# Taking the value and key weights of the second half 512 columns at a time, with another opening and another final sum

## The chip, the cores and the metric

One core of one Trainium2 chip. The metric is the device time of one launch, in microseconds (us): the median over runs of the same kernel. The engines are named as in the profile: PE (TensorE matmul), PEld (its weight load), DVE (VectorE), ACT (ScalarE), POOL (GpSimd) and SP (SyncE, which here issues the DMAs).

## The reference

One layer of a hybrid encoder in fp32, on a prompt of 2048 frames and a sample of 64 frames with 4096 cached ones, 1024 channels.

```python
h = rmsnorm(x, norm_g) @ w_in                     # 1024 -> 6144 columns
qa, ka, va, za, qb, kb, vb, zb, ga, gb = split(h) # 512 each, ga and gb 1024
# branch A: 4 heads, two 64-wide parts each, softmax(p0) - lam * softmax(p1), ALiBi, chunk mask
oa = diff_attention(rmsnorm(qa), rmsnorm(ka), va)
# branch B: 4 heads of retention, chunks of 64, a decaying state
ob, state = retention(qb, kb * 128 ** -0.5, vb)
m = sigmoid(ga + b0) * ((rms(oa) * silu(za)) @ w_oa) + sigmoid(gb + b1) * ((rms(ob) * silu(zb)) @ w_ob)
y = x + m @ w_out
```

The outputs are y for prompt and sample, the new keys and values, and the retention states.

## The kernel before

Every product with x or a weight is done in three fp32r matmuls on split operands: a high part (the cast to fp32r) and a low part (what the cast left off), hi·hi, hi·lo and lo·hi. The high part of a weight piece is cast on ACT (`w_piece`, tiles `wh`), the low part subtracted on POOL, for a few pieces on DVE (`w_low`, tiles `wl`). Pieces come from memory into `ws` tiles (`w_load`), issued on SP's queue.

The prompt is worked in two halves of 1024 rows; half 0 also carries the 64 sample rows. For each half, a stream `w_stream` goes through the columns of `w_in`: values, keys and queries of the attention, values of the retention (`natural`: a tile of 128 rows of x is loaded into PE as the stationary operand, and 256 or 512 columns of weights move past it), then the retention's queries and keys and the gates (`transposed`: weights stationary). Each output tile is handed to finishing work (`spawn_fin`: normalisation, splitting, storing). A second stream, `z_stream`, does the attention of half 0, the attention of the sample, the retention of half 0, and the attention and the retention of half 1. Where `w_stream` is done, `out_stream` follows: `m_tile` (the two output projections with `w_o_diff` and `w_o_ret`, 264 columns a matmul), then `y_quad` (the last product with `w_out`, seven block products instead of eight).

No order is written out for the whole: the streams are generators, and a planner with one clock for each engine, advanced by a cost for each instruction, decides at build time whose next step is emitted. `yield lambda: ...` holds a stream until the condition is met, `yield t` until PE's planned clock has reached t; `take` and `give` take and free one of a limited set of rooms by its tag. So an engine's instructions stand in a fixed order on the chip, and a change of a condition or a cost moves other streams' work too.

Places that the change touches:

- `opening` does the first row tile by a list, `OPENING`: H is x high by weight high, X is x low by weight high, L is x high by weight low, each with one of 8 chunks; T is the transposing of x tile 1 (`x_tile`). `warm(n)` emits n small matmuls on a tile of ones, whose result nobody uses.
- In half 1 of before, `ORD` gives the order of 256-column groups: values 0, keys 0, queries 0, a mark, values 1, keys 1, queries 1, a mark. With 256 columns two row tiles share a tile of 512 columns in PSUM.
- `w_room` says where split weights live: the ordinary rooms ("w", 16), or rooms of the attention ("K", "V") for the wide groups 0 and 2 (values and queries of half 0).
- `head_in` holds the loading of an attention head until the mark of its group has been passed by 9000 ns on PE's planned clock.
- `y_last` ends the kernel: the last block product is split in two halves of 256 columns, each added to `xr` and stored.

Of the kernel before, what the change touches and what calls it, by code (L numbers as in the profile page):

```python
# [45 lines left out]
XFLY = 3  # L46
# [3 lines left out]
OPENING = [(k[0], int(k[1])) for k in ("H0 X0 H1 X1 H2 X2 L0 H3 X3 L1 H4 X4 L2 T1 H5 X5 L3 H6 X6 L4 "  # L50
                                       "H7 X7 L5 L6 L7").split()]
# [20 lines left out]
class Hybrid:  # L72
# [197 lines left out]
    def x_prep(self):  # L270
# [131 lines left out]
    def spread(self):  # L402
# [8 lines left out]
        self.warm(2)  # L411
# [51 lines left out]
    def x_tile(self, j, mid=None):  # L463
# [3 lines left out]
        for q in range(2):  # L467
# [19 lines left out]
            if q == 0 and mid:  # L487
                yield from mid()
# [48 lines left out]
    def w_piece(self, wait):  # L537
# [10 lines left out]
        return self.w_low(wide, n, st, h, l, th, tag, tags)  # L548

    def w_low(self, wide, n, st, h, l, t, tag, tags):  # L550
        th = t
        if n in (5, 7, 8):
# [53 lines left out]
    def opening(self, fin):  # L606
# [16 lines left out]
        self.norm_scale(0)  # L623
        yield lambda: len(self.xin) > 1
# [10 lines left out]
        for _ in range(7):  # L635
# [6 lines left out]
        for k, c in OPENING:  # L642
            if k == "T":
# [42 lines left out]
    def natural(self, half, fin, fresh=False, wide=False):  # L686
        if fresh and wide:
# [319 lines left out]
    def q_loader(self, half):  # L1007
        for h in range(4):
            yield from self.head_in(half, h)
# [3 lines left out]
    def head_in(self, half, h):  # L1013
        k = f"kqv{h // 2}{half}"
        yield lambda: k in self.done
        yield self.marks[k] + 9000

    def h_loader(self, half):
        for h in range(4):
            yield from self.head_in(half, h)  # L1020
# [899 lines left out]
    def y_quad(self, g):  # L1920
# [3 lines left out]
        for k, (bank, b, need, done) in enumerate(SEVEN):  # L1924
# [31 lines left out]
            if split:  # L1956
                for u in range(2):
# [7 lines left out]
                    self.spawn(self.y_last(q, ps, t, cols), 0)  # L1965
# [70 lines left out]
    def y_last(self, q, ps, t, cols):  # L2036
        yield lambda: "x12" in q
        yield max(t, q["x12"])
        x = self.xr[q["g"]][0]["12"]
        self.nc.vector.tensor_add(x[:, cols], ps[:, cols], x[:, cols])  # L2040
        yield self.V(256, max(t, self.pe))
# [95 lines left out]
    def w_stream(self):  # L2137
# [12 lines left out]
        first = ([wva, wk, wq, m0, m1], ORD(fva0, fva, fk, fq, m0, m1))  # L2150
# [18 lines left out]
        self.npiece = 0  # L2169
        self.opened = False  # L2170
# [22 lines left out]
    def mark(self, name):  # L2193
        yield lambda: True
        self.done.add(name)
        self.marks[name] = self.pe

    def z_stream(self):
        for half in range(2):
            yield lambda: f"kqv0{half}" in self.done  # L2200
# [143 lines left out]
```

## Time and profile before

| | before |
|---|---|
| median of 3 runs (us) | 1929.06 (1929.06 to 1929.89) |
| the profiled execution, own time / span (us) | 1930.11 / 1928.3 |
| PE, PEld busy (us) | 1919.0, 1709.7 |
| DVE, ACT, POOL busy (us) | 1132.9, 1004.7, 463.8 |
| DMA | 308.50 MB, mean 160 GB/s |

The span is the part of the execution that the profiler covers; the 1.8 us between it and the execution's own time lie around it. Matmuls are pipelined, so that their durations overlap: 100% for PE says that some matmul is always under way, not that PE couldn't do more in the time. The pace is read from the timeline, from one start to the next. In the timeline each row has the start in us, the duration, the engine, the line, the operation, output<-inputs by the program's names, the shape and, in brackets, idle time ahead of it with what ended it.

### The profile page before, as it was taken

The numbers are of one execution on the slowest core, as the hardware profiler recorded it, in microseconds if no ns is written. First come the engines' busy times: TensorE is split into PE (matmuls) and PEld (weight loads), VectorE is DVE, ScalarE is ACT, GpSimd is POOL, SyncE is SP. The second block draws the span as 40 slices with busy tenths as digits, with TensorE's granted clock in tenths as the row PEclk, the third lists the DMA queues.
The fourth block names the chain that finished last, engine by engine and source line by source line (L and its number), as shares of the span: only waits on it lengthen the run. The fifth ranks groups of instructions, "written<-read, shape, count | busy, mean of one in ns | idle before, by whom it ended". The sixth has DMA issues, their size and how long they took to land.

```text
span 1928.3 us, 32935 instructions
## 1 busy us (share of the span) xinstructions
PE 1919.0 (100%) x11626; PEld 1709.7 (89%) x11626; DVE 1132.9 (59%) x2794; ACT 1004.7 (52%) x2137; POOL 463.8 (24%) x365
## 2 busy tenths in 40 slices
PE   9999999999999999999999999999999999999999
PEld 7878899999889999999988888888889889999887
DVE  6553575635565345656856656646664339977664
ACT  6433676655445544545756756645664535554221
POOL 2320121212121223212102211221221526522442
PEclk9999999999999999999999999999999999999999
DMA  7647463425556887664334243363233758886542
GB/s 247 208 149 185 139 182 117 125 84 161 167 158 172 228 230 206 179 195 141 106 104 138 90 129 97 107 190 108 69 115 101 236 167 253 261 247 198 180 153 77
DMA packets 356343, 308.50 MB, mean 160 GB/s; under 512 B 65745, under 2 KB 313809, under 8 KB 356178
## 3 DMA queue, kind: packets, MB, share of 16 engines
q1 hardware_dynamic: 356178, 306.39, 53.5%
q8 instruction: 92, 1.51, 0.3%
q14 instruction: 73, 0.60, 0.1%
HBM read 201.38 MB, written 99.88 MB: 156 GB/s over the span
## 4 chain that ended last, share of the span: by engine, by line
PE 95%; DVE 2%; DMA 1%; ACT 1%; issue 0%; SPq 0%; DVEq 0%; ACTq 0%
PE mm L592 55%; PE s L1066 3%; PE s L1067 3%; PE at L1174 3%; PE pv L1154 2%; PE pv L1153 2%; PE pv L1152 2%; PE s L1949 1%; PE s L1951 1%; PE s L1950 1%; PE pv L1420 1%; PE pv L1533 1%; PE at L1523 1%; PE tp L789 1%; PE mm L1949 1%; PE mm L1951 1%
## 5 line engine op out<-in xcount | busy, mean ns | idle before, releaser
L592 PE MATMUL mm<-xh,wh 128*128 128x512 f32 (+2 forms) x1280 | 457.5, 357 | 0.0
L592 PE MATMUL mm<-xh,wl 128*128 128x512 f32 (+2 forms) x1280 | 452.4, 353 | 0.0
L592 PE MATMUL mm<-xl,wh 128*128 128x512 f32 (+2 forms) x1280 | 451.9, 353 | 0.0
L556 POOL TENSOR_TENSOR wl<-ws,wh 128x512 fp32r<-128x512 f32 x189 | 256.7, 1372 | 654.8 <-ACT wh L546 479.0
L592 PEld LDWEIGHTS mm<-xh,wl 128*128 128x128 f32 x1280 | 240.9, 188 | 31.2
L592 PEld LDWEIGHTS mm<-xh,wh 128*128 128x128 f32 x1280 | 241.3, 188 | 29.1
L592 PEld LDWEIGHTS mm<-xl,wh 128*128 128x128 f32 x1280 | 241.3, 189 | 28.9
L592 PE MATMUL mm<-wh,xh 128*128 128x256 f32 (+1 forms) x696 | 235.8, 339 | 0.5 <-ACT raw L754 0.3
L592 PE MATMUL mm<-wh,xl 128*128 128x256 f32 (+1 forms) x696 | 231.1, 332 | 0.0
L592 PE MATMUL mm<-wl,xh 128*128 128x256 f32 (+1 forms) x696 | 230.8, 332 | 0.0
L1189 DVE TENSOR_TENSOR atl<-at,ath 128x512 fp32r<-128x512 f32 (+1 forms) x144 | 93.0, 659 | 146.7 <-ACT ath L1187 146.7
L892 ACT COPY ev<-mm 128x512 f32<-128x512 f32 x140 | 71.2, 509 | 190.6 <-PE mm L592 149.8
L1105 ACT ACTIVATE row<-row,a_mx 128x1024 f32<-128x1024 f32 (+7 forms) x160 | 153.8, 963 | 5.0 <-DVE a_mx L1085 4.8
L1075 DVE CUSTOM_DVE_ANT_0 row<-s,dfar 128x512 f32<-128x512 f32 (+2 forms) x192 | 118.0, 630 | 58.7 <-PE s L1067 58.5
L592 PEld LDWEIGHTS mm<-wh,xh 128*128 128x128 f32 x696 | 131.9, 190 | 14.1 <-ACT raw L754 0.8
L592 PEld LDWEIGHTS mm<-wh,xl 128*128 128x128 f32 x696 | 131.8, 189 | 13.3
L592 PEld LDWEIGHTS mm<-wl,xh 128*128 128x128 f32 x696 | 132.0, 190 | 12.7
L546 ACT CAST wh<-ws 128x512 fp32r<-128x512 f32 x192 | 115.6, 617 | 47.3 <-PE mm L592 24.7
L1187 ACT CAST ath<-at 128x512 fp32r<-128x512 f32 (+1 forms) x144 | 78.5, 564 | 100.5 <-PE at L1174 97.5
L955 POOL TENSOR_TENSOR r_y<-r_y,r_sq 128x256 f32<-128x256 f32 x33 | 24.7, 748 | 426.0 <-DVE r_sq L952 164.3
L1066 PE MATMUL s<-K,q 128*128 128x512 f32 (+3 forms) x320 | 119.4, 377 | 0.0
L1067 PE MATMUL s<-K,q 128*128 128x512 f32 (+3 forms) x320 | 115.6, 363 | 0.0
(387 smaller groups left out, 4180.9 us busy)
## 6 DMA issues: line engine op xcount, KB each, us to landing
ws<-in_w_in_dram SPq DMA_DIRECT2D x192, 256.0 KB, 3.1
q<-qT SPq DMA_DIRECT2D x128, 128.0 KB, 3.0
V<-vN SPq DMA_DIRECT2D x24, 512.0 KB, 5.6
K<-kT SPq DMA_DIRECT2D x48, 256.0 KB, 4.2
xt<-in_x_prompt_dram SPq DMA_DIRECT2D x16, 512.0 KB, 5.5
kn<-in_cache_k_T_dram SPq DMA_DIRECT2D x32, 256.0 KB, 3.4
vc<-in_cache_v_diff_dram SPq DMA_DIRECT2D x32, 256.0 KB, 3.3
mT<-mo SPq DMA_DIRECT2D x64, 128.0 KB, 3.1
```

Source lines behind the costliest of these rows:

```text
L546: self.nc.scalar.copy(h, st)
L556: self.nc.gpsimd.tensor_sub(l, st, h.bitcast(F32))
L592: nc.tensor.matmul(ps, p, q, start=c == 0 and i == 0, stop=c == KC - 1 and i == 2)
L892: nc.scalar.copy(ev, ps)
L1066: nc.tensor.matmul(ps, q1s, kk, start=True, stop=False)
L1067: nc.tensor.matmul(ps, q2s, kk, start=False, stop=True)
L1075: nc.vector.tensor_tensor_reduce(out=units[k0 // 1024][:, k0 % 1024:k0 % 1024 + n], in0=ps, in1=tab, scale=-SLOPES[h], scalar=3.0e38, op0= ...
L1105: nc.scalar.activation(u, u, AF.Exp, bias=mx, scale=-1.0, accum_out=lp[:, k:k + 1])
L1152: nc.tensor.matmul(o, v0, ah[:, s0:s0 + n], start=kt == 0, stop=False)
L1174: nc.tensor.transpose(at[:, w:w + 128], src, self.ident)
L1187: nc.scalar.copy(ah[:, :w], at[:, :w])
L1189: nc.vector.tensor_sub(al[:, :w], at[:, :w], ah[:, :w].bitcast(F32))
```

## The change

1. In half 1, values and keys are each one group of 512 columns (`wva`, `wk`), with the queries in two groups of 256 behind them. The order is values, keys, mark `kv1`, queries 0, mark `q01`, queries 1, mark `q11`. The wide values' weights live in the attention's rooms, and wait until the attention of the sample no longer needs its own (`n_spv == 4`).
2. `head_in` waits for the mark of what it needs (for half 1 `kv1` for keys and values, `q01` or `q11` for queries), and besides until all finishing work that was spawned ahead of that mark has ended (`fins`, `before`).
3. Odd pieces of the queries' weights in half 1 have their low parts made on DVE.
4. The opening: two weight pieces are loaded ahead of x tile 1, its list begins with two H products and has single filler matmuls (W), and `warm` is called for three instead of two, and for three more behind the first x tile; x tile 1 is normalised behind it.
5. The final sum: `y_last` is called at once after each half of the columns, no longer spawned.

```diff
-OPENING = [(k[0], int(k[1])) for k in ("H0 X0 H1 X1 H2 X2 L0 H3 X3 L1 H4 X4 L2 T1 H5 X5 L3 H6 X6 L4 "
-                                       "H7 X7 L5 L6 L7").split()]
+OPENING = [(k[0], int(k[1])) for k in ("H0 H1 W1 X0 X1 L0 L1 W1 H2 X2 H3 X3 H4 X4 L2 T1 H5 X5 L3 "
+                                       "L4 H6 X6 H7 X7 L5 L6 L7").split()]
...
# x_prep
-            yield lambda: self.xfly < XFLY and (j < 2 or self.wloads >= 8)
+            yield lambda: self.xfly < XFLY and self.wloads >= (0, 2, 8)[min(j, 2)]
...
# w_load
+                    if self.wloads == 2:
+                        yield lambda: len(self.xin) > 1
...
# w_room
-        elif nw in (0, 2):
+        elif nw in (0, 2, 4):
+            if nw == 4:
+                yield lambda: self.n_spv == 4
             tags, pool, shape = ("K", "V"), self.ap, [128, 2, 512]
...
-        return self.w_low(wide, n, st, h, l, th, tag, tags)
+        return self.w_low(wide, n in (5, 7, 8) or not wide and nw == 6 and q % 2, st, h, l, th, tag, tags)
...
# opening
+        for _ in range(2):
+            low.append((yield from self.w_piece(False)))
+        for g in low:
+            yield from g
+        yield from self.x_tile(0)
+        self.warm(3)
         yield lambda: len(self.xin) > 1
         self.norm_sums(1)
+        self.norm_log(1)
         self.norm_mean(1)
-
-        def first():
-            yield from (yield from self.w_piece(False))
-
-        yield from self.x_tile(0, first)
-        self.norm_log(1)
...
# spawn_fin
-        self.spawn(done, 0, "w")
+        self.spawn(self.finish(done, len(self.fins)), 0, "w")
+        self.fins.append(False)
+
+    def finish(self, done, k):
+        yield from done
+        self.fins[k] = True
...
-    def head_in(self, half, h):
-        k = f"kqv{h // 2}{half}"
+    def head_in(self, half, h, names):
+        k = names[half].format(h // 2)
         yield lambda: k in self.done
+        yield lambda: all(self.fins[:self.before[k]])
         yield self.marks[k] + 9000
...
# y_quad, the last product
+                yield lambda: "x12" in q
...
-                    self.spawn(self.y_last(q, ps, t, cols), 0)
+                    self.y_last(q, ps, t, cols)
                     yield self.pe
...
     def y_last(self, q, ps, t, cols):
-        yield lambda: "x12" in q
-        yield max(t, q["x12"])
         x = self.xr[q["g"]][0]["12"]
         self.nc.vector.tensor_add(x[:, cols], ps[:, cols], x[:, cols])
-        yield self.V(256, max(t, self.pe))
+        self.V(256, max(t, q["x12"]))
...
# w_stream
-        first = ([wva, wk, wq, m0, m1], ORD(fva0, fva, fk, fq, m0, m1))
+        first = ([wva, wk, wq, m0, m1], [wva, wk, (None, "kv"), fq[0], (None, "q0"), fq[1], (None, "q1")])
```

How the instructions stand before and after is shown at three places. The names are tiles: `mm`, `s`, `at`, `pv`, `tp` are banks of PSUM, `xh` and `xl` the split x, `ws` a weight piece as loaded, `xt` a tile of x.

The opening on PE (before, then after), from the matmul that spreads the norm's factors over the partitions on; the small matmuls on `ones` are the fillers, the first products are those of `mm`:

```order
L408 MATMUL s<-gz,ones 128x512 x2
L420 MATMUL at<-ones 128x128 x2
L472 MATMUL tp<-ident,xt 128x128 x4
L472 MATMUL pv<-ident,xt 128x128 x4
L656 MATMUL mm<-wh,xh_115 128x512
L656 MATMUL mm<-wh,xl_116 128x512
L656 MATMUL mm<-wh,xh_115 128x512
L656 MATMUL mm<-wh,xl_116 128x512
L656 MATMUL mm<-wh,xh_115 128x512
L656 MATMUL mm<-wh,xl_116 128x512
L656 MATMUL mm<-wl,xh_115 128x512
L656 MATMUL mm<-wh,xh_115 128x512
```

```order
L408 MATMUL s<-gz,ones 128x512 x2
L420 MATMUL at<-ones 128x128 x3
L472 MATMUL tp<-ident,xt 128x128 x4
L472 MATMUL pv<-ident,xt 128x128 x4
L420 MATMUL at<-ones 128x128 x3
L663 MATMUL mm<-wh,xh_115 128x512 x2
L420 MATMUL at<-ones 128x128
L663 MATMUL mm<-wh,xl_116 128x512 x2
L663 MATMUL mm<-wl,xh_115 128x512 x2
L420 MATMUL at<-ones 128x128
L663 MATMUL mm<-wh,xh_115 128x512
```

Fillers now stand behind the transposes of x tile 0 and between the first products, and the first two H products lie ahead of the first two X products.

The opening on SP's queue (before, then after):

```order
L147 DMA xt<-in_x_prompt_dram 128x1024
L147 DMA gz<-in_norm_g_dram 1x1024
L147 DMA ident<-in_c_ident_dram 128x128
L147 DMA xt<-in_x_prompt_dram 128x1024
L147 DMA ws<-in_w_in_dram 128x512 x8
L147 DMA xt<-in_x_prompt_dram 128x1024 x6
```

```order
L147 DMA xt<-in_x_prompt_dram 128x1024
L147 DMA gz<-in_norm_g_dram 1x1024
L147 DMA ident<-in_c_ident_dram 128x128
L147 DMA ws<-in_w_in_dram 128x512 x2
L147 DMA xt<-in_x_prompt_dram 128x1024
L147 DMA ws<-in_w_in_dram 128x512 x6
L147 DMA xt<-in_x_prompt_dram 128x1024 x6
```

Two of the weight pieces have moved ahead of the second tile of x.

The start of half 1 on PE, at the end of the last gate product of half 0 (320 columns; before, then after):

```order
L592 MATMUL mm<-xl_118,wh 128x320
L592 MATMUL mm<-xh_117,wl 128x320
L592 MATMUL mm<-wh,xh_8434 128x256
L592 MATMUL mm<-wl,xh_8434 128x256
L592 MATMUL mm<-wh,xl_8435 128x256
```

```order
L594 MATMUL mm<-xl_118,wh 128x320
L594 MATMUL mm<-xh_117,wl 128x320
L594 MATMUL mm<-wh,xh_8462 128x512
L594 MATMUL mm<-wl,xh_8462 128x512
L594 MATMUL mm<-wh,xl_8463 128x512
```

The same products move past in 512 columns instead of 256. In all, the program has 378 matmuls fewer: 384 go here and 6 fillers come. The attention of half 1 begins later in the order, and `z_stream` ends later. Between its last transpose (the retention's) and the first matmul of `m_tile` stand 342 product matmuls of 512 columns before, and 216 after.

The end on PE, around the thirteenth of the last 24 matmuls (before, then after; in brackets what an instruction waits for):

```order
L1962 MATMUL at<-wb22h,mh 128x256
L1962 MATMUL at<-wb22l,mh 128x256
L1962 MATMUL at<-wb22h,ml 128x256
L1962 MATMUL at<-wb22h,mh 128x256
L1962 MATMUL at<-wb22l,mh 128x256
L1962 MATMUL at<-wb22h,ml 128x256
```

```order
L1976 MATMUL at<-wb22h,mh 128x256
L1976 MATMUL at<-wb22l,mh 128x256
L1976 MATMUL at<-wb22h,ml 128x256
L1976 MATMUL at<-wb22h,mh 128x256 [waits DVE_49]
L1976 MATMUL at<-wb22l,mh 128x256
L1976 MATMUL at<-wb22h,ml 128x256
```

The same place on DVE (before, then after):

```order
L2014 TENSOR_TENSOR cap<-at,cap 128x512 [waits DVE_49]
L2048 TENSOR_TENSOR xr<-mm,xr 128x512 [waits DMAHW1_49,PE_49]
L2048 TENSOR_TENSOR xr<-s,xr 128x512 [waits DMAHW2_49,PE_49,Pool_49]
L2040 TENSOR_TENSOR xr<-at,xr 128x256 [waits PE_49,Pool_49]
L2040 TENSOR_TENSOR xr<-at,xr 128x256
```

```order
L2028 TENSOR_TENSOR cap<-at,cap 128x512 [waits DVE_49]
L2060 TENSOR_TENSOR xr<-mm,xr 128x512 [waits DMAHW1_49,PE_49]
L2052 TENSOR_TENSOR xr<-at,xr 128x256 [waits PE_49,Pool_49]
L2060 TENSOR_TENSOR xr<-s,xr 128x512 [waits DMAHW2_49]
L2052 TENSOR_TENSOR xr<-at,xr 128x256 [waits PE_49]
```

The thirteenth matmul now waits for DVE; on DVE the add of the first half stands ahead of the add of the preceding block product (`xr<-s`), and the second half's behind it.

More of the change, by code (lines that the diff above doesn't have):

```diff
@@ L547, in w_piece, with w_low @@
         th = self.A(512, max(self.pe, t))
-        return self.w_low(wide, n, st, h, l, th, tag, tags)
-    def w_low(self, wide, n, st, h, l, t, tag, tags):
+        return self.w_low(wide, n in (5, 7, 8) or not wide and nw == 6 and q % 2, st, h, l, th, tag, tags)
+    def w_low(self, wide, vector, st, h, l, t, tag, tags):
         th = t
-        if n in (5, 7, 8):
+        if vector:
             self.nc.vector.tensor_sub(l, st, h.bitcast(F32))
@@ L623, in opening @@
         self.norm_scale(0)
+        for _ in range(2):
[3 more added lines that the diff above has]
+        yield from self.x_tile(0)
+        self.warm(3)
         yield lambda: len(self.xin) > 1
         self.norm_sums(1)
+        self.norm_log(1)
         self.norm_mean(1)
-        def first():
-            yield from (yield from self.w_piece(False))
-        yield from self.x_tile(0, first)
-        self.norm_log(1)
         self.norm_root(1)
         self.norm_scale(1)
-        for _ in range(7):
+        low = []
+        for _ in range(6):
             low.append((yield from self.w_piece(False)))
@@ L642, in opening @@
         for k, c in OPENING:
+            if k == "W":
+                self.warm(c)
+                continue
             if k == "T":
@@ L686, in natural @@
     def natural(self, half, fin, fresh=False, wide=False):
-        if fresh and wide:
+        if fresh and wide and half == 0:
             yield from self.opening(fin)
@@ L1008, in q_loader @@
         for h in range(4):
-            yield from self.head_in(half, h)
+            yield from self.head_in(half, h, ("kqv{}0", "q{}1"))
             for p in range(4 * half, 4 * half + 4):
                 yield from self.load_q(h, p)
-    def head_in(self, half, h):
-        k = f"kqv{h // 2}{half}"
+    def head_in(self, half, h, names):
+        k = names[half].format(h // 2)
         yield lambda: k in self.done
+        yield lambda: all(self.fins[:self.before[k]])
         yield self.marks[k] + 9000
@@ L1019, in h_loader @@
         for h in range(4):
-            yield from self.head_in(half, h)
+            yield from self.head_in(half, h, ("kqv{}0", "kv1"))
             yield from self.load_head(half, h)
@@ L2169, in w_stream @@
         self.npiece = 0
+        self.n_spv = 0
+        self.fins, self.before = [], {}
         self.opened = False
@@ L2196, in mark @@
         self.marks[name] = self.pe
+        self.before[name] = len(self.fins)
     def z_stream(self):
         for half in range(2):
-            yield lambda: f"kqv0{half}" in self.done
+            yield lambda: ("kqv00", "kv1")[half] in self.done
             if half == 0:
```

5 lines of the change are left out of this document (1 added, 4 removed).

## The prediction

> **What bounds the kernel now.** I read the page first: the span, the busy shares and the chain that ended last.
>
> ```profile
> span 1928.3 us, 32935 instructions
> ...
> PE 1919.0 (100%) x11626; PEld 1709.7 (89%) x11626; DVE 1132.9 (59%) x2794; ACT 1004.7 (52%) x2137; POOL 463.8 (24%) x365
> ...
> PE 95%; DVE 2%; DMA 1%; ACT 1%; issue 0%; SPq 0%; DVEq 0%; ACTq 0%
> ```
>
> PE carries 95% of the chain and is busy from one end to the other, so only two things can move the end: what PE's instructions cost, and the few places where PE stands still. Those are in the waits of PE, longest first (us in total, times, longest).
>
> ```profile
> PE mm L656 <- ACT wh L546: 1.8, 2, 1.1
> PE at L420 <- DVE epst L2268: 1.1, 1, 1.1
> PE at L1823 <- DVE ogl L1779: 0.9, 1, 0.9
> ```
>
> The first is in the opening, where product matmuls wait for the cast of their weights; the second is the start of the program. Behind these three no wait is over 0.5 us. A busy PE says little about its pace, since matmuls overlap: durations in the groups are about twice the distance from one start to the next. So I price every matmul by that distance, from PE's timeline.
>
> **Part 1, the wide products of the second half.** Both halves of the value and key weights of half 1 were taken 256 columns at a time. The group of 256-column matmuls by shape is:
>
> ```profile
> L592 PE MATMUL mm<-wh,xh 128*128 128x256 f32 x384 | 110.8, 289 | 0.2 <-DVE tlo L835 0.2
> ```
>
> With its two sisters (wh·xl and wl·xh, as many each) that is 1152 matmuls for value, key and query: 8 row tiles, 8 chunks of the inner dimension, 3 products and 6 blocks of columns. Value and key are two thirds, 768; the change makes 384 of 512 columns of them. The pace of the 256s, at the start of half 1 (24 in a row, of which the first and the last are shown):
>
> ```profile
> 739.05 0.28 PE L592 MATMUL mm<-wh,xh 128*128 128x256 f32 x1
> ...
> 741.81 0.28 PE L592 MATMUL mm<-wh,xl 128*128 128x256 f32 x1
> ```
>
> 2.76 us over 23 steps is 0.1200 us. The same product at 512 columns exists in half 0: values with their weights in the attention's rooms (from the second row to the third 22 steps), and keys with weights in the ordinary rooms (14 steps).
>
> ```profile
> 55.21 0.48 PE L592 MATMUL mm<-wh,xh 128*128 128x512 f32 x1
> 55.53 0.40 PE L592 MATMUL mm<-wl,xh 128*128 128x512 f32 x1
> ...
> 60.66 0.40 PE L592 MATMUL mm<-wh,xl 128*128 128x512 f32 x1
> ```
>
> ```profile
> 84.67 0.39 PE L592 MATMUL mm<-wh,xh 128*128 128x512 f32 x1
> ...
> 87.85 0.39 PE L592 MATMUL mm<-wh,xl 128*128 128x512 f32 x1
> ```
>
> That is 5.13/22 = 0.2332 and 3.18/14 = 0.2271 us. Before: 768 × 0.1200 = 92.2. After: 192 × 0.2332 + 192 × 0.2271 = 88.4. The saving is 3.8 us; if both go at the slower pace it is 2.6, if both at the faster 5.0. I take the rooms as they correspond.
>
> The Trainium skill, "TensorE: Matmul & The Clock Gate", section "Wait — 56ns, not 53.3ns?", puts the start-to-start distance at N columns / 2.4 GHz plus about 2.5 ns; by it a pair of 256s exceeds a 512 by 2.5 ns only, and 384 pairs save 1.0 us by estimate. This trace disagrees with it in size (0.2400 against 0.2271 to 0.2332, 7 to 13 ns a pair) and the measurement decides.
>
> Small against it: the first product matmul behind a transpose lies 55.53 − 55.21 = 0.32 from its successor instead of 0.233, and the changed order has 225 such switches for 222, so 3 × 0.09 = 0.25 us more.
>
> **Part 2, the opening.** Windows of PE's granted clock (us, busy time and count of PE, PEld, DVE, ACT, POOL, then the clock and the DMA), and PE's timeline there:
>
> ```profile
> 9.23:12.65 3.42, 1.87 (x7) 1.20 (x8) 2.68 (x8) 3.39 (x9) 2.39 (x2) 1.00 1.01 375
> 12.65:16.06 3.41, 3.41 (x11) 2.62 (x10) 3.41 (x4) 1.94 (x4) 3.41 (x4) 0.50 1.03 418
> 16.06:19.47 3.41, 3.41 (x19) 2.88 (x18) 3.30 (x6) 2.64 (x7) 1.39 (x1) 1.00 1.02 408
> ```
>
> ```profile
> 10.10 0.50 PE L656 MATMUL mm<-wh,xh 128*128 128x512 f32 x1 [1.08 <-ACT wh L546]
> ...
> 11.52 0.50 PE L656 MATMUL mm<-wh,xh 128*128 128x512 f32 x1 [0.69 <-ACT wh L546]
> ...
> 12.98 0.63 PE L656 MATMUL mm<-wh,xh 128*128 128x512 f32 x1
> 13.41 0.63 PE L656 MATMUL mm<-wh,xl 128*128 128x512 f32 x1
> ...
> 18.55 0.86 PE L656 MATMUL mm<-wl,xh 128*128 128x512 f32 x3
> 19.25 0.40 PE L592 MATMUL mm<-wh,xh 128*128 128x512 f32 x1
> ```
>
> PE idles 1.08 + 0.69 = 1.77 us in the first of these windows, and the clock is 0.50 throughout the next, where matmuls stand 13.41 − 12.98 = 0.43 apart. The first row tile ends where L592 begins, at 19.25. After the change two weight pieces are queued on SP ahead of x tile 1 (512 KB), so the first two casts no longer stand behind it; filler matmuls and two H products cover the idle stretch, and only some 0.3 us of idle is left in the window by my walk through the new order. Then the clock stays at 1.00. What is late next is the last low piece, on DVE:
>
> ```profile
> 13.23 4.77 DVE L553 TENSOR_TENSOR wl<-ws,wh 128x512 fp32r<-128x512 f32 x3
> ```
>
> Three in 4.77 us end at 18.0. Before, PE was later still: three L products remained at 18.55 and ended at 19.25. After, with no halved window, only the last L product (0.23) is left when the last low piece comes. I put that at 17.5, half a us earlier than 18.0: the queue brings the same bytes, and only x tile 1's work ahead on DVE is a little out of the way. So L592's place is reached at 17.7, a gain of 1.5 us. Bounds: nothing, if the clock halves all the same; 1.77 + 3.41/2 = 3.5, if no low piece held PE up. The six additional fillers lie in idle time.
>
> The Trainium skill, same page, section "What's actually happening", says the window of the gate is free-running: with another phase, the same gaps may fall into two windows. No row here shows another phase; it makes the bound of nothing a rival.
>
> **Part 3, the final sum.** The last product has 24 matmuls of 256, twelve for each half of the columns; then two adds and their stores (PE, DVE, and the queue of SP):
>
> ```profile
> 1922.75 0.28 PE L1962 MATMUL at<-wb22h,ml 128*128 128x256 f32 x1
> 1922.87 0.28 PE L1962 MATMUL at<-wb22h,mh 128*128 128x256 f32 x1
> ...
> 1924.16 0.28 PE L1962 MATMUL at<-wb22h,ml 128*128 128x256 f32 x1
> ```
>
> ```profile
> 1921.70 0.69 DVE L2048 TENSOR_TENSOR xr<-s,xr 128x512 f32<-128x512 f32 x1 [2.17 <-DMA out_y_prompt_dram<-xr]
> 1924.55 0.76 DVE L2040 TENSOR_TENSOR xr<-at,xr 128x256 f32<-128x256 f32 x2 [2.16 <-PE at L1962]
> ```
>
> ```profile
> 1918.88 6.93 SPq L152 DMA_DIRECT2D out_y_prompt_dram<-xr  x5
> ```
>
> Before, the thirteenth matmul (1922.87) follows the twelfth at once, and both adds wait for the twenty-fourth. After, the first half's add is issued between the halves, and the thirteenth matmul, which writes the same tile, waits for it. By the rows: the twelfth ends at 1922.75 + 0.28 = 1923.03; an add starts 0.11 behind its product (1924.16 + 0.28 = 1924.44, add at 1924.55), takes 0.76/2 = 0.38 and ends at 1923.52; with the same 0.11 PE resumes at 1923.63, a stall of 0.76. The second half ends 11 × 0.118 + 0.28 = 1.58 later, at 1925.21, its add at 1925.70, against 1925.31 before: +0.4 us. The add of the preceding product (1921.70, 0.69) is now queued on DVE behind the first half's add, at 1923.52 to 1924.21: out of the way of the last one, but its 256 KB store leaves 2.5 us later. Bounds: −0.4, if the last store lands faster alone than two together, to +0.8, if it queues behind that store.
>
> **Part 4, what waits.** Odd pieces of the second-half query weights are split on DVE instead of POOL, heads wait for all finishing work of their group, and the wide values wait for the attention's rooms. From keys to queries all 16 weight rooms are full until the last key tile, so the query's low pieces come just in time; the nearest row is the DVE low piece above, 4.77/3 = 1.6 us, if one is late altogether, and nothing if none is. I take 0.3 for all transitions, bounds 0 to 2. Values have tens of us of lead and the head waits hold a stream that has other work beside it: nothing.
>
> The stream of attention and retention ends later. In the order there are 342 product matmuls of 512 columns between its last transpose and the first output projection; now 216, or 216 × 0.2271 = 49 us. Before:
>
> ```profile
> 1493.83 0.60 PE L1573 MATMUL tp<-ident,rvx 128*128 128x128 f32 x4
> ```
>
> ```profile
> 1571.82 0.28 PE L1822 MATMUL s<-ogh,w_o_diffh 128*128 128x264 f32 x1
> ```
>
> ```profile
> 1504.47 0.88 DVE L1630 TENSOR_TENSOR w_o_diffl<-wst,w_o_diffh 128x512 fp32r<-128x512 f32 x1 [14.35 <-DMA wst<-in_w_o_ret_dram]
> ...
> 1537.98 1.56 DVE L1630 TENSOR_TENSOR w_o_retl<-wst,w_o_reth 128x512 fp32r<-128x512 f32 x1 [1.39 <-ACT w_o_reth L1623]
> 1546.02 2.46 DVE L1768 TENSOR_TENSOR on<-on,z 128x528 f32<-128x528 f32 x2 [6.48 <-ACT z L1765]
> 1551.46 0.71 DVE L1768 TENSOR_TENSOR on<-on,z 128x528 f32<-128x528 f32 x1 [2.98 <-ACT z L1765]
> ...
> 1573.23 0.71 DVE L1768 TENSOR_TENSOR on<-on,z 128x528 f32<-128x528 f32 x1 [10.18 <-ACT z L1765]
> ```
>
> The stream ended at 1493.83 + 0.60 = 1494.43, and the stretch was 1571.82 − 1494.43 = 77.4 us. The output weights need their splits in it, the last of which ended at 1537.98 + 1.56 = 1539.54, 45.1 us behind the stream's end. 49 still covers 45.1, so I count nothing; the margin falls from 32 us to 4.
>
> **The sum**, against the profiled execution (span 1928.3, its own time 1930.11, so 1.05 above the median of 1929.06): −3.8 + 0.25 − 1.5 + 0.4 + 0.3 = −4.35. Span 1923.95, profiled time 1925.8, median 1924.7. A measurement can tell about 0.2% here, 3.9 us, so faster begins below 1925.2.
>
> **The rivals.** *The clock halves all the same* (18%): the opening gives nothing, −2.85, 1926.2. For it: the granted clock stays at 0.50 for a whole window on 1.55 us less of PE work; against it: fillers where the idle time was.
>
> *The pair saves next to nothing* (7%): the tail's 256s stand 0.118 apart (1922.75 to 1922.87). If the pace of 0.120 came from other work beside them, and all 512s go at 0.2332, the saving is 768 × 0.118 − 384 × 0.2332 = 1.1, and the time 1927.4. Against it: the two paces were measured with the same other stream beside both. The skill's page named in part 1 would put it there too.
>
> *Everything goes well* (15%): both wide products at 0.2271 (−5.0), opening −2.5 (half way from 1.5 to its bound), tail 0, no late piece: −5.0 + 0.25 − 2.5 = −7.25, 1921.8.
>
> *The second stream ends too late* (8%), the one on the other side. The splits began 10.0 us behind its end (1504.47), waiting for the loads into rooms that it frees. If those loads meet the weight stream and take twice as long, the need is 55.1, PE stands for 6 us, and work for DVE that was done in the last 29 us of the stretch (the last three rows of DVE above: 2.46 + 4 × 0.71 = 5.3 us) falls into a stage whose DVE is full:
>
> ```profile
> 1574.00:1594.00 20.00, 20.00 (x167) 20.00 (x166) 13.01 (x30) 11.44 (x26) 7.26 (x8) 1.00 0.88 268
> ...
> 1614.00:1634.00 20.00, 20.00 (x166) 20.00 (x165) 19.63 (x39) 12.55 (x28) 12.49 (x12) 1.00 0.86 253
> ```
>
> With 19.59 to 19.76 of 20 us busy it has no room, so 5.3 more: −4.35 + 11.4 gives 1936.1. It decides the sign from a need of 49 + 4.35 = 53.4 us on. Against it: the order of that work is unchanged, and PE waited for DVE in that stage only 0.9 us.
>
> **The numbers.** My own case has 52%; its spread, 1923.2 to 1926.2, crosses the bound of 1925.2, with some seven tenths below. Faster: 0.7 × 52 + 15 = 51, with a little from the cases between, 53%. Slower: 8%. Within 0.2%: 39%. The range of 8 in 10 reaches from the good case's side, 1921.5, over the clock and the pair cases and 2 us of late pieces, to 1929.0.
>
> **What would show it.** In the changed profile: L594 matmuls of 512 columns in half 1 at 0.227 to 0.233; clock 1.00 in every window of the opening and the first L594 near 17.7; a stall of 0.7 to 0.8 us ahead of the thirteenth of the last 24; no wait over 2 us between keys, queries and values; the first output projection some 49 us behind the last transpose, with no idle ahead of it. A wait of PE of several us anywhere, or a clock of 0.5 beyond the opening, would make the prediction wrong.

## The result: 3.1 us slower, where 4.35 less were forecast

| us | before | after |
|---|---|---|
| median of 22 runs each | 1929.03 (1927.88 to 1931.55) | 1932.09 (1929.82 to 1937.25) |
| profiled execution, own time / span | 1930.11 / 1928.3 | 1930.42 / 1928.6 |

The ratio is 1.0019, 95% interval 1.0013 to 1.0025: slower by 0.19%. Two executions of all, 2692.63 us of before and 4899.04 us of `half1_cast_later`, lie far off the others and are left out of the ratios. The runs spread twice as wide, and the profiled execution of after is among its quickest, so its trace shows less than the median's loss. Its page:

```profile
span 1928.6 us, 32127 instructions
...
PE 1917.4 (99%) x11254; PEld 1688.7 (88%) x11254; DVE 1148.1 (60%) x2798; ACT 1004.0 (52%) x2137; POOL 461.2 (24%) x361
...
PE 92%; DVE 3%; DMA 3%; ACT 1%; SPq 1%; issue 0%; DVEq 0%; ACTq 0%
```

PE is busy for 1.6 us less in a span as long. The chain ran through PE for 95% before and now for 92%, with 3% each through DVE and DMA (2% and 1% before). Work is saved, and waits have come. The longest waits of PE:

```profile
PE s L1079 <- DVE a_acc L1088: 1.7, 1, 1.7
...
PE mm L594 <- ACT ev L904: 0.9, 2, 0.5
...
PE at L1976 <- DVE xr L2052: 0.6, 1, 0.6
```

The first, 1.7 us on `s`, and the fourth, 0.9 us on ACT's `ev`, were not there before, nor was the wait for `xr`, the one forecast in the final sum.

**The opening** came out as worked out, at its own place. The windows of the clock and the first L594:

```profile
9.23:12.65 3.42, 3.13 (x19) 2.45 (x18) 2.55 (x7) 3.35 (x8) 1.46 (x2) 1.00 1.05 402
12.65:16.06 3.41, 3.41 (x20) 2.77 (x20) 3.41 (x4) 3.41 (x7) 3.41 (x3) 1.00 1.03 411
```

```profile
17.83 0.40 PE L594 MATMUL mm<-wh,xh 128*128 128x512 f32 x1
```

Neither window has the clock at 0.50, and the first row tile is done at 17.83 (forecast 17.7; before 19.25), 1.42 us earlier. That is measured against one execution of before, whose clock was halved; the first batch of experiments shows that not every one is.

**The wide products** run at 2.57/11 = 0.2336 us (values, 783.03 to 785.60) and 2.31/10 = 0.2310 (keys, 843.47 to 845.78):

```profile
783.03 0.40 PE L594 MATMUL mm<-wh,xh 128*128 128x512 f32 x1
...
785.60 0.39 PE L594 MATMUL mm<-wh,xl 128*128 128x512 f32 x1
```

```profile
843.47 0.40 PE L594 MATMUL mm<-wl,xh 128*128 128x512 f32 x1
...
845.78 0.39 PE L594 MATMUL mm<-wh,xl 128*128 128x512 f32 x1
```

That makes 192 × (0.2336 + 0.2310) = 89.2 for 92.2 of before, 3.0 us saved where 3.8 were forecast. The two stretches are short: over all 339 steps of under 0.3 us from one such product of half 1 to the next the mean is 0.2316 us, which gives 3.2.

**The final sum** has its stall ahead of the thirteenth matmul, 1923.67 − 1922.80 = 0.87 for 0.12, so 0.75 of stall where 0.76 were worked out, and the last add starts at 1925.40 for a forecast of 1925.21 + 0.11 = 1925.32:

```profile
1922.80 0.28 PE L1976 MATMUL at<-wb22h,ml 128*128 128x256 f32 x1
1923.67 0.39 PE L1976 MATMUL at<-wb22h,mh 128*128 128x256 f32 x1 [0.59 <-DVE xr L2052]
```

```profile
1923.19 0.42 DVE L2052 TENSOR_TENSOR xr<-at,xr 128x256 f32<-128x256 f32 x1 [3.60 <-PE at L1976]
...
1925.40 0.42 DVE L2052 TENSOR_TENSOR xr<-at,xr 128x256 f32<-128x256 f32 x1 [1.19 <-PE at L1976]
```

**The end of the second stream**, the first output projection behind it and the last split of its weights on DVE:

```profile
1523.35 0.60 PE L1586 MATMUL tp<-ident,rvx 128*128 128x128 f32 x4
```

```profile
1572.79 0.28 PE L1835 MATMUL s<-ogh,w_o_diffh 128*128 128x264 f32 x1
```

```profile
1563.81 1.75 DVE L1643 TENSOR_TENSOR w_o_retl<-wst,w_o_reth 128x512 fp32r<-128x512 f32 x1 [2.38 <-ACT w_o_reth L1636]
```

The stretch is 1572.79 − 1523.95 = 48.8 us (forecast 49), and the last split ends at 1563.81 + 1.75 = 1565.56, 41.6 us into it: in time.

So the forecast's own places are near what they should be, and add up to some −4 against the profiled execution of before. The loss had to be elsewhere, in waits that the forecast put at nothing or at 0.3.

### The profile page after: what moved, and what is told of

Same layout as the page of the kernel before. It is cut to its first block, busy times and chain, and to the rows that moved or that the text cites. A ratio compares the mean times of both kernels' runs of the same rounds, so it can differ in the third digit from the quotient of the medians.

```text
span 1928.6 us, 32127 instructions
## 1 busy us (share of the span) xinstructions
PE 1917.4 (99%) x11254; PEld 1688.7 (88%) x11254; DVE 1148.1 (60%) x2798; ACT 1004.0 (52%) x2137; POOL 461.2 (24%) x361
## 4 chain that ended last, share of the span: by engine, by line
PE 92%; DVE 3%; DMA 3%; ACT 1%; SPq 1%; issue 0%; DVEq 0%; ACTq 0%
PE mm L594 53%; PE s L1079 3%; PE s L1080 3%; PE at L1187 3%; PE pv L1167 2%; PE pv L1166 2%; PE pv L1165 2%; DMA xt<-in_x_prompt_dram 1%; PE s L1962 1%; PE s L1964 1%; PE s L1963 1%; PE pv L1546 1%; PE at L1536 1%; PE pv L1433 1%; PE s L1513 1%; PE mm L1962 1%
## 5 line engine op out<-in xcount | busy, mean ns | idle before, releaser
L594 PE MATMUL mm<-xh,wh 128*128 128x512 f32 (+2 forms) x1280 | 458.3, 358 | 0.9 <-ACT ev L904 0.9
L594 PE MATMUL mm<-xh,wl 128*128 128x512 f32 (+2 forms) x1280 | 452.5, 353 | 0.0
L594 PE MATMUL mm<-xl,wh 128*128 128x512 f32 (+2 forms) x1280 | 452.0, 353 | 0.0
L594 PEld LDWEIGHTS mm<-xh,wl 128*128 128x128 f32 x1280 | 240.9, 188 | 31.2
L594 PEld LDWEIGHTS mm<-xh,wh 128*128 128x128 f32 x1280 | 241.3, 189 | 30.4 <-ACT ev L904 1.3
L594 PEld LDWEIGHTS mm<-xl,wh 128*128 128x128 f32 x1280 | 241.4, 189 | 28.8
L594 PE MATMUL mm<-wh,xh 128*128 128x512 f32 (+1 forms) x568 | 214.1, 377 | 0.3 <-ACT raw L766 0.3
L594 PE MATMUL mm<-wh,xl 128*128 128x512 f32 (+1 forms) x568 | 209.2, 368 | 0.1
L594 PE MATMUL mm<-wl,xh 128*128 128x512 f32 (+1 forms) x568 | 208.8, 368 | 0.1
L1118 ACT ACTIVATE row<-row,a_mx 128x1024 f32<-128x1024 f32 (+7 forms) x160 | 153.7, 962 | 8.7 <-DVE a_mx L1098 8.7
L1088 DVE CUSTOM_DVE_ANT_0 row<-s,dfar 128x512 f32<-128x512 f32 (+2 forms) x192 | 118.1, 631 | 52.3 <-PE s L1080 51.6
L1140 DVE SCALAR_TENSOR_TENSOR row<-row,a_w 128x1024 f32<-128x1024 f32 (+4 forms) x96 | 102.1, 1069 | 37.5 <-ACT row L1137 37.4
L594 PEld LDWEIGHTS mm<-wh,xl 128*128 128x128 f32 x568 | 107.0, 188 | 19.6 <-DVE xl L480 0.6
L594 PEld LDWEIGHTS mm<-wh,xh 128*128 128x128 f32 x568 | 107.1, 189 | 17.9 <-ACT raw L766 0.8
L594 PEld LDWEIGHTS mm<-wl,xh 128*128 128x128 f32 x568 | 107.3, 189 | 17.0 <-DVE wl L555 0.3
L1079 PE MATMUL s<-K,q 128*128 128x512 f32 (+3 forms) x320 | 118.7, 376 | 1.7 <-DVE a_acc L1088 1.7
```

Source lines behind the costliest of these rows:

```text
L594: nc.tensor.matmul(ps, p, q, start=c == 0 and i == 0, stop=c == KC - 1 and i == 2)
L1079: nc.tensor.matmul(ps, q1s, kk, start=True, stop=False)
L1088: nc.vector.tensor_tensor_reduce(out=units[k0 // 1024][:, k0 % 1024:k0 % 1024 + n], in0=ps, in1=tab, scale=-SLOPES[h], scalar=3.0e38, op0= ...
L1118: nc.scalar.activation(u, u, AF.Exp, bias=mx, scale=-1.0, accum_out=lp[:, k:k + 1])
L1140: nc.vector.scalar_tensor_tensor(out=u0, in0=u0, scalar=w[:, 0:1], in1=u1, op0=ALU.mult, op1=ALU.add)
```

## The experiments

Medians below are of 6 to 11 runs against 21 to 33 of before in the same batch, 1928.6 to 1929.0. The intervals of the ratios are about 0.001 to either side (1.9 us), so a median's step of 1 us is a hint and 3 us is a finding; the traces decide where they show a wait gone.

**First batch: which part.** Each part of the change was put on, or taken off, by itself. `open_only` is before with item 4 of the change, `half1_undone` with items 4 and 5, `half1_only` with items 1 to 3, and `tail_undone` is after without item 5:

```diff
# tail_undone, against after
-                yield lambda: "x12" in q
...
-                    self.y_last(q, ps, t, cols)
+                    self.spawn(self.y_last(q, ps, t, cols), 0)
```

> The kernel before with the changed opening alone. Theory 1 (the loss lies in the second half, where casts of weights now wait on ACT for rooms ahead of the attention's work): the opening keeps the 1.42 us that the first L594 row gained (17.83 for 19.25), so about 1.4 us below before, 1927.6, and as narrow a spread. Theory 2 (the loss comes from the opening's other order, which shifts loads and heads of half 0): no gain, at or above 1929.

> The change without its second-half part and without the new condition on heads: the opening and the final sum alone. Theory 1: -1.4 from the opening and +0.4 to +0.8 from the final sum, so 1928.0 to 1928.5. Theory 2: as slow as the changed kernel, 1931 to 1932.

> The changed kernel with the final sum as before. Theory 1: 0.4 to 0.8 us faster than the changed kernel, about 1931.5, with the changed kernel's wide spread. If the final sum were harmless, as slow as the changed kernel.

> The kernel before with the second-half part and the condition on heads, with the old opening and the old final sum. Theory 1: the loss is all here, about 1932 to 1933 (the changed kernel's 1932.1 plus 1.4 less 0.5), spread from 1930 to 1937, with waits of PE for DVE and ACT after 900 us. Theory 2: 1925 to 1927, the saving of the wide products.

| | median | ratio, 95% interval |
|---|---|---|
| open_only | 1928.96 | 0.9999 (0.9990 to 1.0008) |
| half1_undone | 1929.10 | 1.0001 (0.9992 to 1.0009) |
| tail_undone | 1931.45 | 1.0012 (1.0003 to 1.0021) |
| half1_only | 1932.48 | 1.0015 (1.0006 to 1.0025) |

The second-half part carries the loss, 1932.48, as theory 1 has it. But the gain of the opening, on which theory 1 counted as well, isn't there: alone the opening gives 0.0, and `half1_undone`, with the final sum as well, stands at before's time too, where 1928.0 to 1928.5 was expected. Two things take the 1.42 us.

*The stores at 37 us.* PE, ACT and SP's queue in `open_only`, then SP's queue in before:

```profile
38.10 0.50 PE L592 MATMUL mm<-wh,xh 128*128 128x512 f32 x1 [0.82 <-ACT xh L479]
```

```profile
34.89 0.59 ACT L836 CAST thi<-mm 128x512 fp32r<-128x512 f32 x1 [5.31 <-DMA vN<-thi]
...
37.48 0.57 ACT L479 CAST xh<-tp 128x512 fp32r<-128x512 f32 x1
```

```profile
29.30 0.43 SPq L147 DMA_DIRECT2D dfar<-in_c_dfar_dram  x1
29.84 0.38 SPq L152 DMA_DIRECT2D vN<-thi  x1
```

```profile
29.36 0.38 SPq L152 DMA_DIRECT2D vN<-thi  x1
...
30.75 0.42 SPq L147 DMA_DIRECT2D dfar<-in_c_dfar_dram  x1
```

ACT stands 5.31 us for the store of an earlier value tile (`vN<-thi`), whose room its cast needs; x's cast (L479) is queued behind, and PE waits for that. In before the store was issued at 29.36 and the attention's table `dfar` behind it (30.75); now `dfar` is ahead (29.30, the store at 29.84). The 97th matmul at L592 starts at 45.08 in `open_only` and at 45.15 in before, so by then the gain of this execution is gone. In after ACT stands 5.17 us at the same place, but PE loses less: the same matmul starts at 44.31.

*The clock of before.* The 1.42 us are measured against a halved clock, and before doesn't always have one. Seven traces have the old opening. In before, `heads_wait_only`, `half1_narrow` and `half1_x_later` one window there has the clock at 0.50, and the first row tile is done at 19.03 to 19.37. In `half1_only`, `half0_heads_early` and `half1_cast_later` none has, and it is done at 17.97 to 18.22, against 17.62 to 17.85 in the nine traces with the new opening. The windows begin at another time in each execution. In before, one of them (9.23 to 12.65) holds nearly all of the two idle stretches, and PE is busy for 1.87 us of it; in `half1_only` the stretches fall into two (7.11 to 10.53 and 10.53 to 13.94), with 2.84 and 2.72 us busy, and the clock stays at 1.00. One halved window lowers the mean clock of an execution by 3.41/2/1928 = 0.0009. Of the 107 executions of before in the four batches of experiments, 47 have a mean clock that is given as 1.000, with a median of 1928.03, and 60 a lower one, with a median of 1929.07; of the 110 with the new opening, those of after among them, 105 have 1.000. So the opening removes a loss of about 1 us which a little over half of the executions of before have.

**Second batch: why.**

```diff
# open_tables_late, against open_only (the same for dnear)
+        self.nc.vector.memset(self.dfar[:, 0:1], 0.0)
         self.ld(self.dfar, self.i["c_dfar"], 1 << 19)
# half0_heads_early, against half1_only
+        if half == 1:
             yield lambda: all(self.fins[:self.before[k]])
# half1_cast_later, against half1_only, in w_piece
+        if wide and nw == 6 and q > 3:
+            yield self.pe + 1500
         self.nc.scalar.copy(h, st)
# half1_narrow, against half1_only
-        first = ([wva, wk, wq, m0, m1], [wva, wk, (None, "kv"), fq[0], (None, "q0"), fq[1], (None, "q1")])
+        first = ([wva, wk, wq, m0, m1], [fva0, fva[1], fk[0], fk[1], (None, "kv"), fq[0], (None, "q0"), fq[1], (None, "q1")])
...
-        elif nw in (0, 2, 4):
+        elif nw in (0, 2):
```

> The changed opening alone, with the two attention tables (dfar, dnear) made to load when the attention starts instead of some 29 us into the kernel (a one-column memset ahead of each load). Theory A: the opening's 1.4 us are lost at 37 us, because dfar is now ahead of the stores of the value tiles on SP's queue, so a tile is freed late and the cast behind it on ACT holds up x: without the tables there, 1927.5 to 1927.9, and no wait of L592 for ACT xh. Theory B: x itself arrives too late for a PE that is 1.4 us earlier: 1929.0 and the wait stays.

> The second-half part alone, but the heads of half 0 are loaded without waiting for the finishing work (those of half 1 still wait). Theory A: that condition moves the attention of half 0 by 9 us and the sample's end by 28 us, onto the loads of x for half 1, whose squares on ACT then wait for DMA ahead of the sample's casts: without it the waits near 352 and 676 go, 1929 to 1930.5. Theory B: the order of the second half itself is what costs: 1932.5 as before.

> The second-half part alone, with the last four casts of the retention's value weights in half 1 emitted 1.5 us later on the planned clock. Theory A: the wait of 1.7 us near 929 (PE for DVE a_acc) comes of such a cast, which stands on ACT ahead of the attention's exponentials and waits for PE to free a room: it shrinks or goes, 1930.6 to 1931.5. Theory B: the pieces are late anyway and PE waits for them instead: 1932.5.

> The second-half part alone with its order, marks and conditions, but values and keys of half 1 as two groups of 256 columns each, in the ordinary rooms, and no low pieces on DVE. Theory A (the wide groups do save about 3 us, order and conditions cost 6): 1933 to 1936. Theory B (the wide groups and their rooms cost): 1929 to 1931.

| | median | ratio, 95% interval |
|---|---|---|
| open_tables_late | 1928.11 | 0.9995 (0.9986 to 1.0005) |
| half0_heads_early | 1928.40 | 1.0000 (0.9990 to 1.0009) |
| half1_cast_later | 1933.68 | 1.0025 (1.0015 to 1.0035) |
| half1_narrow | 1934.31 | 1.0028 (1.0017 to 1.0039) |

*Tables late.* The waits of PE in the first 100 us, `open_only`, then `open_tables_late`:

```profile
PE at L420 <- DVE epst L2273: 1.1, 1, 1.1
PE mm L592 <- ACT xh L479: 0.8, 1, 0.8
```

```profile
PE at L420 <- DVE epst L2275: 1.1, 1, 1.1
PE mm L661 <- ACT wh L546: 0.3, 1, 0.3
```

The wait for `xh` is gone, so the tables' place on the queue made it. The time fell by 0.85, less than the 1.4 expected and within the interval. The executions of before with a mean clock of 1.000 have a median of 1928.61 in this batch (12 of them) and of 1928.03 in all (47), beside 1928.11 here. So the rest of the 1.4 is likely the halved clock, and against a before at full clock the opening is worth some half a us or less; the runs don't tell it more exactly.

*Heads early* takes back 4.1 us by the medians (2.9 by the ratios), the whole loss, by one condition in half 0. The largest of the waits that it removes, in the trace of `half1_only` on ACT and then on PE, with ACT of before:

```profile
673.97 1.06 ACT L320 ACTIVATE xt<-xt 128x1024 f32<-128x1024 f32 x1 [2.65 <-DMA xt<-in_x_prompt_dram]
...
675.59 0.36 ACT L1457 CAST atp<-at 128x256 fp32r<-128x256 f32 x1
```

```profile
677.32 1.61 PE L1428 MATMUL pv<-vhl,atp 128*128 128x256 f32 x8 [1.45 <-DVE atp L1459]
```

```profile
662.63 0.21 ACT L1449 CAST atp<-at 64x64 fp32r<-64x64 f32 x1
...
671.12 1.04 ACT L320 ACTIVATE xt<-xt 128x1024 f32<-128x1024 f32 x1
```

The square of x for half 1 (L320) stands on ACT waiting 2.65 us for its load. Behind it are the casts of the sample's attention (L1457), DVE needs them, and PE stands 1.45 us. In before the sample's casts are done by then, and no square waits. With the condition the first head's first product starts at 209.21 in `half1_only`, for 202.00 in before, and the sample's last product at 697.40 for 665.88, in the time of those loads. The same square waits 2.65 us here, 1.04 in after and 0.42 in `heads_wait_only` below. The runs spread less without the condition (1927.75 to 1930.74, against 1928.94 to 1934.19); that waits on loads make the spread fits this, but isn't shown. The Trainium skill, "PSUM — Partial Sum Buffer", section "Engine vs sequencer instructions", says that the queues of ScalarE, VectorE and GpSimd are strictly first in, first out; the trace agrees here.

*Cast later* goes against theory A: the wait near 929 is replaced by two others of 1.2 us each, one of them for the low piece on POOL, and the kernel is 1.2 us slower by the medians. *Narrow* hints that widening, with its rooms and the low pieces on DVE, is worth having, by 1.8 us.

**Third batch: the condition alone, the meeting of loads and sample, and a mended kernel.** `combined` is after with three changes: `half0_heads_early`'s line, late tables, and the final sum of before.

```diff
# heads_wait_only, against before (fins and before as in the change)
+        if half == 0:
+            yield lambda: all(self.fins[:self.before[k]])
# half1_x_later, against half1_only
-                if half == 0 and k == len(seqs[0]) - 4:
+                if half == 0 and k == len(seqs[0]) - 3:
# combined_d14000, against combined, in head_in
-        yield self.marks[k] + 9000
+        yield self.marks[k] + (9000 if half == 0 or k == "kv1" else 14000)
```

> The kernel before with one thing added: the heads of half 0 wait until the finishing work of their groups has ended. Theory A (this condition is what costs, by the sample's attention sliding onto the loading of x for half 1 and by the wait near 352): about 4 us slower than before, 1932 to 1933.5, with waits near 352 and 676. Theory B (it costs only together with the wide groups): 1929 to 1930.

> The second-half part alone with the loading and normalising of x for half 1 started one group of gates later. Theory A: the squares of x no longer wait on ACT ahead of the sample's casts, the waits at 676 and 684 go, 1930.5 to 1931.5 against 1932.5, narrower. Theory B: those waits have another cause: 1932.5.

> The change with three parts mended: heads of half 0 do not wait for finishing work, the attention tables load late, the final sum is as before. By the parts so far (1928.4 for the second half with early heads, -0.8 for the opening with late tables): 1927.2 to 1928.0, faster than before by about 1.3; the wait near 926 stays. If the parts' gains hide each other: 1928.5 or more.

> The same, with the queries of half 1 loaded 14000 ns instead of 9000 behind their mark, so that the first head's exponentials lie differently to the casts that wait for rooms. Theory A (the 1.7 us near 926 is the meeting of those casts and the first head on ACT): the wait shrinks, 1925.5 to 1927. Theory B (the pieces are late whatever stands beside them): no better than the kernel without it, 1927.5 or slower.

| | median | ratio, 95% interval |
|---|---|---|
| heads_wait_only | 1933.92 | 1.0029 (1.0017 to 1.0040) |
| half1_x_later | 1931.72 | 1.0016 (1.0008 to 1.0025) |
| combined | 1927.62 | 0.9995 (0.9986 to 1.0004) |
| combined_d14000 | 1925.66 | 0.9987 (0.9978 to 0.9996) |

The condition alone costs 5.3 us on the kernel of before, which settles that it is the cause. The clock of the opening doesn't make these differences: a mean below 1.000 have 3 of 6 executions here and 15 of 28 of before, as 4 of 11 of `half1_only` and 5 of 11 of `half0_heads_early`. Its waits from 200 to 900 us:

```profile
PE pv L1159 <- ACT ath L1194: 1.3, 1, 1.3
PE mm L592 <- DVE tlo L840: 0.9, 1, 0.9
PE tp L794 <- DVE raw L779: 0.8, 1, 0.8
```

Before had none over 0.5 us there. The first of these, which ends at 354.54, was in `half1_only` too; the next two (they end at 878.95 and 810.36) were not, and the squares of x wait only 0.9 us in this execution and stop PE for none of them. So the condition costs by several waits, in changing shares; that the sum is 4 to 5 us is shown by the times, the share of each isn't. For half 1 the condition was left in place in every run, since heads might read keys there that aren't stored yet; what it costs in half 1 is open. The wait near 353 is the same pattern: in the trace of after ACT waits there 2.62 us for the store of an attention output, then the cast comes that PE needs. Moving x's loading (`half1_x_later`) took the waits at 676 and 684 away, but one of 2.5 us came at 897, with a window of clock 0.50 behind it (899.73 to 903.14), and little was gained; this trace is of the slowest of its runs, 1935.81.

The wait near 929, on ACT, DVE, POOL and PE of after:

```profile
925.07 0.62 ACT L548 CAST wh<-ws 128x512 fp32r<-128x512 f32 x1 [1.37 <-issue]
925.60 1.15 ACT L1118 ACTIVATE row<-row,a_mx 128x1024 f32<-128x1024 f32 x1
```

```profile
913.71 0.69 DVE L786 TENSOR_TENSOR raw<-raw,sm_y 128x512 f32<-128x512 f32 x1
...
925.79 1.83 DVE L786 TENSOR_TENSOR raw<-raw,sm_y 128x512 f32<-128x512 f32 x1
927.54 1.24 DVE L1128 TENSOR_TENSOR a_ls<-a_lp 128x1 f32<-128x1 f32 x1
...
928.89 1.11 DVE L1128 TENSOR_TENSOR a_ls<-a_lp 128x1 f32<-128x1 f32 x1
...
930.32 0.42 DVE L1088 CUSTOM_DVE_ANT_0 row<-s,dnear 128x256 f32<-128x256 f32 x1
```

```profile
925.77 1.30 POOL L558 TENSOR_TENSOR wl<-ws,wh 128x512 fp32r<-128x512 f32 x1 [20.96 <-DVE sm_y L251]
927.42 2.57 POOL L558 TENSOR_TENSOR wl<-ws,wh 128x512 fp32r<-128x512 f32 x2 [0.35 <-ACT wh L548]
```

```profile
930.80 0.50 PE L1079 MATMUL s<-K,q 128*128 128x512 f32 x1 [1.70 <-DVE a_acc L1088]
```

A cast of the retention's value weights waits on ACT for PE to leave a room (1.37 us idle; the row says `issue`, since it is ACT's sequencer that stands on PE's semaphore, which goes up at 925.00). The first head's exponentials (L1118) are queued behind it. But this is not what holds DVE up: the last of their sums (`a_lp`) that L1128 needs is there at 927.85. What holds DVE up is POOL, which with this cast and the two behind it gets three pieces to split. L786 takes 1.83 us beside the first of these, instead of its 0.69 (at 913.71). The two L1128, of one column each, take 1.24 and 1.11 us beside the other two and end within 0.02 us of them (POOL's at 928.77 and 929.99). The 48 instances of L1128 in this trace beside which POOL does nothing take 0.14 to 0.16. That is 1.14 + 1.09 + 0.96 = 3.2 us more on DVE, and behind it stands L1088, which frees `s` for PE: 1.70 us. L1088 itself reads PSUM, and at 512 columns takes at most 0.69 us in all 47 instances beside POOL's work. The Trainium skill, "SBUF — State Buffer", section "SBUF: two separate sides", says that the port pair which DVE and GpSimd share is an exclusive lock for a whole instruction, and that a DVE operation with two inputs in SBUF needs it against a GpSimd operation that reads SBUF; the trace agrees, by the ends of the two L1128.

Two other waits above are of this kind. In `heads_wait_only` DVE's L250 and L251, of 8 columns, take 1.19 us each at 807.07 and 808.29, beside three splits from 805.61 to 809.47 (0.17 each in after, at 913.30 and 913.50), and PE waits until 810.36. In `half1_x_later` L251 and L781 take 1.14 and 1.71 us at 897.08 and 898.25, beside splits from 896.91 on, ahead of the wait of 2.5 us.

Loading the queries 5 us later moves the head against the casts and splits: in `combined_d14000` the multiplication takes 0.69 us (at 929.76) and the two sums 0.15 and 0.14 (930.98 and 931.25). The waits from 800 to 1000, `combined`, then `combined_d14000`:

```profile
PE s L1082 <- DVE a_acc L1091: 1.7, 1, 1.7
PE tp L801 <- DVE raw L786: 0.5, 1, 0.5
```

```profile
PE tp L801 <- DVE raw L786: 0.6, 1, 0.6
```

The wait is gone and 1.96 us with it by the medians. That the casts and the first head meet is as theory A has it; that they meet on ACT is not, since the time is lost on DVE beside POOL. This version is faster than before, by 0.13%.

**Fourth batch: what widening is worth.** `mended_narrow` is `combined_d14000` with the edit of `half1_narrow`.

> The kernel combined_d14000 with values and keys of half 1 in groups of 256 columns, in the ordinary rooms and without low pieces on DVE. What widening alone is worth, where no other wait stands beside it: by the starts of the 512s in the changed trace 768 x 0.1200 - 192 x 0.2336 - 192 x 0.2310 = 3.0 us, so 1928.5 to 1929; by the comparison of half1_narrow with half1_only 1.8 us, so 1927.3 to 1927.7.

> combined_d14000 on the same chip, so that the two can be compared: 1925.0 to 1926.3, as before; the mended changed kernel, faster than before by 2.5 to 4 us.

Measured: 1927.78 (0.9995, 0.9986 to 1.0004) and 1926.26 (0.9986, 0.9977 to 0.9995), a difference of 1.5 us; by the spans, 1925.2 and 1922.9, 2.3. With 256 columns PE has no wait from 700 to 1000; with 512 it waits at the passage from keys to queries (0.5 us in this batch's trace, 0.6 in the last fence). So 3.0 us by the pace become about 2 with the switches (0.25) and that wait. This is the worth of widening together with its rooms and the low pieces on DVE, which the edit takes off too.

## Why the prediction was wrong

The forecast was 1924.7, −4.35; the measured change is +3.1, and 1932.1 lies outside the range of 1921.5 to 1929.0. By the steps of the sum:

- *Part 1, −3.8*: mechanism right, size off. The pace gives −3.0 to −3.2, since the keys went at 0.2310 and not at 0.2271 in the stretch shown; net of what it brings, 1.5 to 2.3.
- *Part 2, −1.5*: right at its place (1.42), wrong for the kernel. I priced the opening to its first L592 and did not follow the 1.4 us on: at 37 us the store queue takes them back, through SP's order, which the change moved. And I took the halved window of one execution for a lasting cost of before, of which only some half of the executions have it. The traces with another phase, of which I had none, are `half1_only`, `half0_heads_early` and `half1_cast_later`. (Of the 1.77 us idle 1.55 lay in the window.) Alone the opening is worth 0.0, with the tables out of the way 0.85.
- *Part 3, +0.4*: the stall was right to 0.01 us; tail_undone puts it at 0.6, within the noise.
- *Part 4, "the head waits hold a stream that has other work beside it: nothing"*: this is the step that failed. The condition on the heads of half 0 costs 4.1 us in the second-half part and 5.3 alone. It moves the first head by 7 us and the sample's end by some 30. I asked who waits behind the held stream on PE, and not with whom it then meets on ACT, and on DVE beside POOL. Which of its waits costs how much stays open.
- *Part 4, 0.3 for all transitions*: 1.96 us at the values of the retention, plus 0.5 to 0.6 at keys to queries. I looked for pieces that come late for their products. The pieces of the retention's values came in time; but while POOL split them, DVE's work for the first head stood for 3.2 us.
- *The margin of 4 us for the output weights* held: 48.8 us for a need of 41.6.

The rival on the slow side was another mechanism than the one that came. The clock rival fell, since the clock of the new opening stayed at 1.00; that before's own clock stays there too, in nearly half of its executions, was not among the rivals.

## What to carry to other kernels

A condition that holds a stream back moves all that follows, and what counts is whom it then meets on each engine that works its queue in order: a wait for a load or a room, at the head of ACT, delays every instruction behind it, whoever they belong to. Nor is an engine alone because its queue is its own: DVE operations on two operands in SBUF stood here until POOL's split had ended. A gain at the start of a kernel has to be followed through the first things behind it (here the stores). And a cost that one trace shows may not be there in every execution: a second trace, or the clocks of all runs, would have shown that before the forecast.

## What I had not expected of the hardware

The same DVE multiplication took 1.83 us beside a POOL subtraction and 0.69 without it, and a sum of one column 1.24 instead of 0.15. A matmul of 512 columns went at 0.2271 to 0.2336 us by where it stood, while the 256s stood at 0.118 to 0.120. With the old opening the clock was halved after a window in which PE was busy for 1.89 of 3.41 us or less, and not after one with 2.20.
